# Loading the rows of decay sums into tiles of their own, one group ahead

## The chip, the cores and the metric

The kernel runs on one core of a Trainium2 chip. The metric is the device time of one execution in microseconds (us). Three executions of the kernel before took 1480.74, 1482.68 and 2030.02 us; their median is 1482.68 us. The profiled execution took 1480.76 us.

## The reference

Two layers, each a SwiGLU feed-forward at half step, a mixing block, and a second feed-forward. The sequence has 256 positions, the model 1024 channels, all in float32. The mixing block runs an SSD branch (32 heads of 64 channels, 4 groups that share B and C) and a latent attention branch (8 heads) on the same input. What the change touches is the decay of the SSD branch:

```python
acum = jnp.cumsum(dtc * a_g, axis=1)
seg = acum[:, :, None] - acum[:, None, :]
decay = jnp.exp(jnp.where(causal, seg, -jnp.inf))
cb = jnp.einsum('btgn,bsgn->btsg', cc, bc)
xdt = xc * dtc[..., None]
y_diag = jnp.einsum('btsg,btsgh,bsghp->btghp', cb, decay, xdt)
```

The kernel treats the 256 positions as two blocks of 128 without a carried state: the matrix of decays between position s (on the partitions) and position t (along the free axis) has a 128x256 part for s in the first block and a 128x128 part for s in the second, 384 columns together.

## The kernel before, in words

Weights stream from HBM in blocks of up to 128x1024 (`ahead`, L144 to L155): SyncE loads a block into `st`, ScalarE rounds it to a high part `wh` (L152), VectorE forms the rest `wl` (L153), and TensorE multiplies with both. Four blocks are kept ahead. ScalarE therefore stands in the way of every weight block, beside all activations; it takes its instructions strictly in order, and so do the other engines. A wait at the head of ScalarE's queue holds back the roundings of later blocks, the activations of the convolutions and the softmax of attention.

The order of instructions on each engine is set when the program is built: `schedule_with_timeline_sim=True` (L904) lets a planner go through the program with costs of its own and place each instruction where its model says that it can start. A changed wait moves instructions on all engines in the mixing stage.

The mixing stage (`mix`, L418) computes the running sums `acum` (L529), turns them so that each head is a row, copies the 32 rows into `aT` (L535, L536: the 256 sums, and the last 128 once more), writes them to a DRAM tensor `rows` (L538) from GpSimd's queue, and goes through `loop_order` (L130): eight rounds j = 0 to 7, each with a pair of xs convolutions, `ssd(j)`, one attention head `head(j)`, and at every second round B and C of a group (`bc`), `query` and `keyval`.

`spread(j)` (L618) loads the rows of the four heads of round j, two heads at a time, spread over all partitions, into tiles `dec` of 128x2x384, of which there are two. Both loads stand on GpSimd's queue, which has nothing else to do in this stage. `ssd(j)` (L627) then works in place: ScalarE takes Relu of (own sum minus row) (L647, four instructions to a tile), then Exp (L648), VectorE multiplies with the masked C·B product `cbm` (L649), and TensorE multiplies with `xdt` (L655, 16 matmuls in a round). Only then are the tiles free, and `spread(j + 1)` follows at L657. A load of the next round thus waits for L655 of this round, and the Relus of the next round wait for the load.

Around it: `t` (L598) is the tanh of a convolution, `BC` (L599) its result for B and C, L606 the C·B product on TensorE, `cbm` (L609) its masked form. `peT` (L770) and `qkT` (L761, L762) are the operands of attention's scores, `pp` (L791) its probabilities, L802 the product with v. `tm` (L465) holds decay inputs and rotary keys after their transposition.

Of the kernel before, what the change touches and what calls it, by code (L numbers as in the profile page):

```python
# [11 lines left out]
F32 = mybir.dt.float32  # L12
# [3 lines left out]
AF = mybir.ActivationFunctionType  # L16
ALU = mybir.AluOpType

P = 128
L = 2  # L20
T = 256
# [5 lines left out]
NH = 32  # L27
# [33 lines left out]
class Build:  # L61
# [356 lines left out]
    def mix(self, l, X0, Xn, gain, gain_next):  # L418
        nc, v = self.nc, self.vec[l]
        tt, ts, stt = nc.vector.tensor_tensor, nc.vector.tensor_scalar, nc.vector.scalar_tensor_tensor  # L420
        act = nc.scalar.activation
# [40 lines left out]
        pt = self.sps()  # L462
        for c in range(2):
            nc.tensor.transpose(pt[:, c * P:(c + 1) * P], dk[:, c * P:(c + 1) * P], self.ident)
        tm = self.tmp("tm", [P, 2, P], bufs=1)  # L465
        for c in range(2):
            act(out=tm[:, c, :], in_=pt[:, c * P:(c + 1) * P], func=AF.Copy, scale=Rt[:, c:c + 1])
        latent(4)
# [42 lines left out]
        q = self.tmp("dtq", [P, 2, 32], bufs=1)  # L511
# [17 lines left out]
        acum = self.tmp("acum", [P, 2, 32], bufs=1)  # L529
        nc.vector.tensor_copy(acum, pa[:, :64].rearrange("p (c h) -> p c h", c=2))  # L530
        pT = self.sps()
        for c in range(2):
            nc.tensor.transpose(pT[:32, c * P:(c + 1) * P], acum[:, c, :], self.ident)
        aT = self.tmp("aT", [P, 3 * P], bufs=1)[:32]
        nc.scalar.copy(aT[:, :T], pT[:32, :T])  # L535
        nc.scalar.copy(aT[:, T:], pT[:32, P:T])  # L536
        rows = self.dram.tile([NH, 3 * P], F32, name=f"rows{l}")
        nc.gpsimd.dma_start(rows, aT)  # L538

        S = dict(l=l, X=X, A=A, acum=acum, rows=rows, dth=dth, Rf2=Rf2, ef=ef, Rfac=Rfac,  # L540
                 Rckv=Rc[:, 2:4], kpr=kpr, v=v)
# [75 lines left out]

    def spread(self, S, j):  # L618

        S["dec"] = []  # L620
        for q in range(2):
            h = 4 * j + 2 * q
            r = self.tmp("dec", [P, 2, 3 * P])
            self.nc.gpsimd.dma_start(r, S["rows"][h:h + 2, :].unsqueeze(0).to_broadcast([P, 2, 3 * P]))
            S["dec"].append(r)

    def ssd(self, S, j):  # L627
        nc = self.nc
        tt = nc.vector.tensor_tensor
        act = nc.scalar.activation  # L630
        xs, cbm = S["xs", j], S["bc", j // 2]
        h0 = 4 * j
        px = self.sps()
        for c in range(2):
            for i in range(2):
                nc.tensor.transpose(px[:, c * T + i * P:c * T + (i + 1) * P], xs[:, i, c * P:(c + 1) * P], self.ident)
        xdt = self.tmp("xdt", [P, 2, T], bufs=1)
        for c in range(2):
            tt(out=xdt[:, c, :].rearrange("p (h d) -> p h d", d=64),
               in0=px[:, c * T:(c + 1) * T].rearrange("p (h d) -> p h d", d=64),  # L640
               in1=S["dth"][:, c, h0:h0 + 4].unsqueeze(2).to_broadcast([P, 4, 64]), op=ALU.mult)
        dec = S["dec"]
        for q, r in enumerate(dec):
            for i in range(2):
                h = h0 + 2 * q + i
                for c, o, n in ((0, 0, T), (1, T, P)):
                    act(out=r[:, i, o:o + n], in_=r[:, i, o:o + n], func=AF.Relu, scale=-1.0, bias=S["acum"][:, c, h:h + 1])  # L647
            act(out=r, in_=r, func=AF.Exp, scale=-1.0)  # L648
            tt(out=r, in0=r, in1=cbm.unsqueeze(1).to_broadcast([P, 2, 3 * P]), op=ALU.mult)  # L649
        py = self.sps()  # L650
        for q, r in enumerate(dec):
            for c, o, n in ((0, 0, T), (1, T, P)):
                for i in range(2):
                    f = (2 * q + i) * 64
                    nc.tensor.matmul(py[64 * i:64 * i + 64, q * T + c * P:(q + 1) * T], lhsT=xdt[:, c, f:f + 64],  # L655
                                     rhs=r[:, i, o:o + n], start=q == 0 and c == 0, stop=q == 1 and c == 1)
        if j < 7:  # L657
            self.spread(S, j + 1)
        yv = self.tmp("yv", [P, 2, T], bufs=1)
        for i in range(2):  # L660
            nc.vector.scalar_tensor_tensor(out=yv[:, i, :], in0=xs[:, i, :], scalar=self.Dh[:, 2 * j + i:2 * j + i + 1],
                                           in1=py[:, i * T:(i + 1) * T], op0=ALU.mult, op1=ALU.add)
        S["yv", j] = yv
# [245 lines left out]
```

## Time and profile before

| | |
|---|---|
| profiled execution | 1480.76 us |
| its span | 1479.0 us |
| TensorE busy | 1452.7 us (98%) |
| VectorE busy | 1115.0 us (75%) |
| ScalarE busy | 912.0 us (62%) |
| GpSimd busy | 18.6 us (1%) |
| mixing stage of the first layer | about 220 to 475 us |
| mixing stage of the second layer | about 940 to 1210 us |

TensorE works through nearly the whole span. Its idle time and its clock are what a change can win back or lose, so the waits of TensorE and the granted clock (PEclk) are read first, and from each gap one goes back to what was late.

### The profile page before, as it was taken

What the parts mean: (1) busy time and instruction counts of PE and PEld (TensorE: products, weight loads), DVE (VectorE), ACT (ScalarE), POOL (GpSimd) and SP (SyncE); (2) the same over time, 40 slices, a digit from 0 to 9 for tenths busy, and PEclk for the clock granted to TensorE, in tenths of its full rate; (3) what the DMA queues carried; (4) which work ended last, traced back from release to release, by engine and by line L of the source; (5) the groups of instructions that cost most, each with busy time, mean ns of one, the idle gap of its engine ahead of it and who ended that gap; (6) DMA issues with size and microseconds to landing.
All of it is one profiled execution on the core that took longest, in us unless ns stands there. A gap on an engine that the chain in (4) does not pass through costs nothing.

```text
span 1479.0 us, 24986 instructions
## 1 busy us (share of the span) xinstructions
PE 1452.7 (98%) x9418; PEld 1305.6 (88%) x9418; DVE 1115.0 (75%) x2080; ACT 912.0 (62%) x1740; POOL 18.6 (1%) x38
## 2 busy tenths in 40 slices
PE   7999999999999999999999999999899999999999
PEld 6888899888888998888888888998798899988888
DVE  7887678977867677777677776889786776787764
ACT  6655566987875456555455554779777654555542
POOL 0000000000000000000000000000000000000000
PEclk9999999999999999999999999999999999999999
DMA  7555655544544655556655566556444555555563
GB/s 261 188 192 168 206 178 189 179 157 132 185 154 157 200 179 186 190 188 184 194 189 189 192 180 195 175 184 192 139 160 138 164 178 186 185 184 190 192 193 111
DMA packets 75977, 265.65 MB, mean 180 GB/s; under 512 B 8880, under 2 KB 11184, under 8 KB 75856
## 3 DMA queue, kind: packets, MB, share of 16 engines
q1 hardware_dynamic: 73232, 251.37, 52.6%
q0 software_dynamic: 2624, 12.68, 2.7%
q8 instruction: 74, 1.21, 0.3%
q14 instruction: 47, 0.39, 0.1%
HBM read 262.87 MB, written 1.15 MB: 179 GB/s over the span
## 4 chain that ended last, share of the span: by engine, by line
PE 87%; DVE 4%; issue 4%; DMA 3%; ACT 2%; POOL 0%; SPq 0%; POOLq 0%; ACTq 0%; DVEq 0%
PE g L178 40%; PE g L179 20%; PE g L169 7%; PE g L170 7%; PE g L171 7%; DMA dec<-rows 2%; DVE wl L153 1%; PE g L694 1%; PE s L655 1%; PE h L779 1%; PE g L718 1%; DVE cy L595 1%; PE h L778 1%; ACT dec L647 1%; ACT wh L152 1%
## 5 line engine op out<-in xcount | busy, mean ns | idle before, releaser
L152 ACT CAST wh<-st 128x1024 fp32r<-128x1024 f32 (+2 forms) x488 | 500.7, 1027 | 475.4 <-PE g L178 309.9
L153 DVE TENSOR_TENSOR wl<-st,wh 128x1024 fp32r<-128x1024 f32 (+2 forms) x488 | 581.3, 1192 | 261.6 <-ACT wh L152 257.9
L178 PE MATMUL g<-X,wh 128*128 128x512 f32 x928 | 326.5, 395 | 7.8 <-DVE X L205 7.4
L178 PE MATMUL g<-A,wh 128*128 128x512 f32 x938 | 327.6, 395 | 0.0
L179 PE MATMUL g<-X,wl 128*128 128x256 f32 x928 | 261.4, 282 | 0.5 <-DVE wl L153 0.5
L179 PE MATMUL g<-A,wl 128*128 128x256 f32 x938 | 260.5, 278 | 0.0
L178 PE MATMUL g<-oT,wh 128*128 128x512 f32 x704 | 244.5, 392 | 0.0
L169 PE MATMUL g<-X,wh 128*128 128x256 f32 x768 | 221.8, 290 | 3.4 <-DVE cy L595 2.9
L170 PE MATMUL g<-X,wh 128*128 128x256 f32 x768 | 220.9, 288 | 0.0
L171 PE MATMUL g<-X,wl 128*128 128x256 f32 x768 | 220.1, 287 | 0.0
L178 PEld LDWEIGHTS g<-X,wh 128*128 128x128 f32 x928 | 174.3, 188 | 47.2 <-DVE X L205 8.1
L178 PEld LDWEIGHTS g<-A,wh 128*128 128x128 f32 x938 | 175.7, 188 | 40.1
L179 PE MATMUL g<-oT,wl 128*128 128x256 f32 x704 | 196.9, 280 | 0.0
L179 PEld LDWEIGHTS g<-X,wl 128*128 128x128 f32 x928 | 175.9, 190 | 1.6 <-DVE wl L153 0.8
L179 PEld LDWEIGHTS g<-A,wl 128*128 128x128 f32 x938 | 176.6, 188 | 0.4
L178 PEld LDWEIGHTS g<-oT,wh 128*128 128x128 f32 x704 | 131.6, 187 | 28.6
L169 PEld LDWEIGHTS g<-X,wh 128*128 128x128 f32 x768 | 148.6, 194 | 6.2 <-DVE cy L595 4.1
L170 PEld LDWEIGHTS g<-X,wh 128*128 128x128 f32 x768 | 149.0, 194 | 0.6 <-issue 0.5
L171 PEld LDWEIGHTS g<-X,wl 128*128 128x128 f32 x768 | 148.8, 194 | 0.5 <-issue 0.5
L179 PEld LDWEIGHTS g<-oT,wl 128*128 128x128 f32 x704 | 133.0, 189 | 0.2
L171 PE MATMUL g<-oT,wl 128*128 128x256 f32 x272 | 76.8, 285 | 0.0
L170 PE MATMUL g<-oT,wh 128*128 128x256 f32 x272 | 76.7, 283 | 0.0
(287 smaller groups left out, 1831.2 us busy)
## 6 DMA issues: line engine op xcount, KB each, us to landing
st<-in_w_dram SPq DMA_DIRECT2D x238, 512.0 KB, 4.4
st<-in_win_dram SPq DMA_DIRECT2D x124, 512.0 KB, 4.1
st<-in_wso_dram SPq DMA_DIRECT2D x32, 512.0 KB, 3.7
st<-in_w_dram SPq DMA_DIRECT2D x32, 384.0 KB, 3.2
dec<-rows POOLq DMA_DIRECT2D x32, 384.0 KB, 5.4
st<-in_wmo_dram SPq DMA_DIRECT2D x16, 512.0 KB, 3.5
st<-in_wo_dram SPq DMA_DIRECT2D x16, 512.0 KB, 3.4
st<-in_wuq_dram SPq DMA_DIRECT2D x16, 384.0 KB, 3.2
```

Of the source, the lines that this page charges most:

```text
L152: self.nc.scalar.copy(wh, st)
L153: self.nc.vector.tensor_tensor(out=wl, in0=st, in1=wh.bitcast(F32), op=ALU.subtract)
L169: mm(out, lhsT=wh[:, k, :], rhs=xh, start=start and k == 0, stop=False)
L170: mm(out, lhsT=wh[:, k, :], rhs=xl, start=False, stop=False)
L171: mm(out, lhsT=wl[:, k, :], rhs=xh, start=False, stop=stop and k == nk - 1)
L178: mm(out, lhsT=wh[:, k, :], rhs=X[:, x0 + k, :], start=start and k == 0, stop=False)
L179: mm(out[:, :T], lhsT=wl[:, k, :], rhs=X[:, x0 + k, :T], start=False, stop=stop and k == nk - 1)
L595: nc.vector.scalar_tensor_tensor(out=y[:, i, k:], in0=ps[:, :T - k], scalar=v[:, w0 + 3 - k:w0 + 4 - k], in1=y[:, i, k:], op0=ALU.mult, op ...
L647: act(out=r[:, i, o:o + n], in_=r[:, i, o:o + n], func=AF.Relu, scale=-1.0, bias=S["acum"][:, c, h:h + 1])
L655: nc.tensor.matmul(py[64 * i:64 * i + 64, q * T + c * P:(q + 1) * T], lhsT=xdt[:, c, f:f + 64], rhs=r[:, i, o:o + n], start=q == 0 and c = ...
L694: nc.tensor.matmul(pc[c], lhsT=aa, rhs=ww, start=k == 0 and i == 0, stop=k == 3 and i == 2)
L718: nc.tensor.matmul(pc[c], lhsT=aa, rhs=ww[:, k, :], start=k == 0 and i == 0, stop=k == 1 and i == 2)
```

## The change

The rows of round j + 1 no longer land in the tiles in which round j still computes. They land in two tiles `row` of 128x2x256. ScalarE's Relus read `row` and write `dec`, and `spread(j + 1)` stands right behind the activations and multiplications of round j, ahead of its matmuls. A load now waits only for the Relus that read its tile. The Relus themselves, which write `dec`, now wait for the matmuls of the round before, where the load did so earlier. The rows are 256 long in place of 384; the Relu of the second part reads columns 128 to 255 of the same row. Two scratch tiles are dropped: `tm` uses the buffer of `qkT`, `aT` that of `pp`.

```diff
-        tm = self.tmp("tm", [P, 2, P], bufs=1)
+        tm = self.tmp("qkT", [P, 2, T], bufs=1)[:, :, :P]
...
-        aT = self.tmp("aT", [P, 3 * P], bufs=1)[:32]
-        nc.scalar.copy(aT[:, :T], pT[:32, :T])
-        nc.scalar.copy(aT[:, T:], pT[:32, P:T])
-        rows = self.dram.tile([NH, 3 * P], F32, name=f"rows{l}")
+        aT = self.tmp("pp", [P, 3 * P], bufs=1)[:NH, :T]
+        nc.scalar.copy(aT, pT[:NH, :T])
+        rows = self.dram.tile([NH, T], F32, name=f"rows{l}")
...
-        S["dec"] = []
+        S["row"] = []
         for q in range(2):
             h = 4 * j + 2 * q
-            r = self.tmp("dec", [P, 2, 3 * P])
-            self.nc.gpsimd.dma_start(r, S["rows"][h:h + 2, :].unsqueeze(0).to_broadcast([P, 2, 3 * P]))
-            S["dec"].append(r)
+            r = self.tmp("row", [P, 2, T])
+            self.nc.gpsimd.dma_start(r, S["rows"][h:h + 2, :].unsqueeze(0).to_broadcast([P, 2, T]))
+            S["row"].append(r)
...
-        dec = S["dec"]
-        for q, r in enumerate(dec):
+        dec = []
+        for q, row in enumerate(S["row"]):
+            r = self.tmp("dec", [P, 2, 3 * P])
+            dec.append(r)
             for i in range(2):
                 h = h0 + 2 * q + i
                 for c, o, n in ((0, 0, T), (1, T, P)):
-                    act(out=r[:, i, o:o + n], in_=r[:, i, o:o + n], func=AF.Relu, scale=-1.0, bias=S["acum"][:, c, h:h + 1])
+                    act(out=r[:, i, o:o + n], in_=row[:, i, c * P:], func=AF.Relu, scale=-1.0, bias=S["acum"][:, c, h:h + 1])
             act(out=r, in_=r, func=AF.Exp, scale=-1.0)
             tt(out=r, in0=r, in1=cbm.unsqueeze(1).to_broadcast([P, 2, 3 * P]), op=ALU.mult)
+        if j < 7:
+            self.spread(S, j + 1)
...
-        if j < 7:
-            self.spread(S, j + 1)
```

The planner then moves instructions in the mixing stages. Three places matter below. In the changed kernel the lines from L536 on stand one to three numbers off: the Relu is L648, Exp L649, the matmuls of `ssd` L658, tanh L597, `peT` L771, attention's scores L779 to L781.

First place: ScalarE's order around the Relus of round 4 in the first layer, with what each instruction waits for (PE, DVE, Activation: an engine; DMASW: a load from GpSimd's queue; DMAHW: one from SyncE's). Before:

```order
L703 COPY qn<-g 128x256
L770 COPY peT<-h 128x512 [waits PE_49]
L647 ACTIVATE dec<-dec,acum 128x256 [waits DMASW1_49]
...
L647 ACTIVATE dec<-dec,acum 128x256 [waits DMASW2_49]
...
L648 ACTIVATE dec<-dec 128x768 [waits Activation_49]
L598 ACTIVATE t_3770<-cy 128x512 [waits DVE_49]
L648 ACTIVATE dec<-dec 128x768 [waits Activation_49]
```

And in the changed kernel:

```order
L771 COPY peT<-h 128x512 [waits PE_49]
L682 ACTIVATE zz<-zz 128x512 [waits DVE_49]
L703 ACTIVATE ta,ss<-g 128x192 [waits Activation_49] x2
L704 COPY qn<-g 128x256
L152 CAST wh<-st 128x1024 [waits DMAHW0_49,PE_49]
L591 ACTIVATE cy<-g,vec_87 128x256 [waits PE_49]
L597 ACTIVATE t_3777<-cy 128x512 [waits DVE_49]
L648 ACTIVATE dec<-row,acum 128x256 [waits DMASW1_49,PE_49]
...
L648 ACTIVATE dec<-row,acum 128x256 [waits DMASW2_49,PE_49]
...
L649 ACTIVATE dec<-dec 128x768 [waits Activation_49] x2
```

The tanh `t` of B and C and one rounding `wh`, which stood behind the Relus, now stand ahead of them; the Relus wait for TensorE too.

Second place: TensorE's order at the attention head of round 3 in the first layer, around the matmuls of `ssd(3)`. Before:

```order
L655 MATMUL s<-dec,xdt 64x256 x2
L655 MATMUL s<-dec,xdt 64x128 x2
L769 MATMUL h<-cb,qp 128x128 x2
L769 MATMUL h<-cb,kp 128x128 x2
L778 MATMUL h<-qkT 128x128
L779 MATMUL h<-peT 128x128
L778 MATMUL h<-qkT 128x256
```

And in the changed kernel (24 matmuls of one weight block stand where the dots are):

```order
L770 MATMUL h<-cb,qp 128x128 x2
L770 MATMUL h<-cb,kp 128x128 x2
L779 MATMUL h<-qkT 128x128
L169 MATMUL g<-X,wh 128x256
...
L171 MATMUL g<-X,wl 128x256
L780 MATMUL h<-peT 128x128
L779 MATMUL h<-qkT 128x256
L780 MATMUL h<-peT 128x256
L781 LDWEIGHTS identb
L781 MATMUL h<-negb,identb 128x2x128
L658 MATMUL s<-dec,xdt 64x256 x2
```

The matmuls of `ssd(3)` moved from ahead of the attention scores to behind them, and a weight block's matmuls came in ahead of the first one that needs `peT`.

Third place: ScalarE's order at the first Relus of the first layer. Before:

```order
L152 CAST wh<-st 128x1024 [waits DMAHW4_49,PE_49]
L592 ACTIVATE cy<-g,vec_87 128x256 [waits PE_49]
L152 CAST wh<-st 128x768 [waits DMAHW5_49,PE_49]
L647 ACTIVATE dec<-dec,acum 128x256 [waits DMASW1_49]
L647 ACTIVATE dec<-dec,acum 128x128
```

And in the changed kernel:

```order
L152 CAST wh<-st 128x1024 [waits DMAHW4_49,PE_49]
L591 ACTIVATE cy<-g,vec_87 128x256 [waits PE_49]
L648 ACTIVATE dec<-row,acum 128x256 [waits DMASW1_49]
L648 ACTIVATE dec<-row,acum 128x128
L648 ACTIVATE dec<-row,acum 128x256
L648 ACTIVATE dec<-row,acum 128x128
L152 CAST wh<-st 128x768 [waits DMAHW5_49,PE_49]
```

One rounding of a weight block for `query` fell behind the first four Relus.

## Rows read from the trace of the kernel before

**Rows 1.** The page: busy time of the engines, share of the span, instructions.

```profile
PE 1452.7 (98%) x9418; PEld 1305.6 (88%) x9418; DVE 1115.0 (75%) x2080; ACT 912.0 (62%) x1740; POOL 18.6 (1%) x38
```

**Rows 2.** Waits of TensorE: releaser, us in total, times, longest us.

```profile
PE s L606 <- DVE BC L599: 4.4, 2, 3.5
PE h L802 <- ACT pT L800: 3.3, 1, 3.3
PE g L169 <- DVE cy L595: 2.9, 2, 2.4
```

**Rows 3.** Timeline of TensorE: start, us, operation [idle before it <- releaser].

```profile
320.69 0.49 PE L778 MATMUL h<-qkT 128*128 128x128 f32 x2 [1.22 <-ACT peT L770]
330.02 0.70 PE L606 MATMUL s<-BC 128*128 128x256 f32 x2 [0.98 <-DVE BC L599]
337.13 0.70 PE L802 MATMUL h<-pT,vv 128*128 128x256 f32 x2 [3.33 <-ACT pT L800]
1060.80 0.70 PE L606 MATMUL s<-BC 128*128 128x256 f32 x2 [3.46 <-DVE BC L599]
1120.05 0.58 PE L169 MATMUL g<-X,wh 128*128 128x256 f32 x1 [2.37 <-DVE cy L595]
```

**Rows 4.** Busy time by stretch, granted clock (PEclk); the last stretch for comparison.

```profile
338.10:341.50 3.40, 3.40 (x18) 3.40 (x17) 3.28 (x11) 1.83 (x4) 0.00 (x0) 0.50 0.45 148
1061.80:1065.20 3.40, 3.40 (x16) 3.15 (x15) 2.63 (x5) 2.81 (x5) 0.00 (x0) 0.51 0.05 14
1119.80:1123.20 3.40, 3.15 (x15) 3.15 (x15) 3.40 (x8) 1.81 (x9) 0.00 (x0) 0.50 0.49 169
300.00:303.40 3.40, 3.40 (x31) 3.40 (x30) 3.22 (x7) 2.06 (x6) 0.00 (x0) 1.00 0.63 221
```

**Rows 5.** Timeline of ScalarE, Relus of round 4, first layer.

```profile
320.01 0.63 ACT L770 COPY peT<-h 128x512 f32<-128x512 f32 x1
324.72 1.49 ACT L647 ACTIVATE dec<-dec,acum 128x256 f32<-128x256 f32 x4 [4.08 <-DMA dec<-rows]
326.49 1.50 ACT L647 ACTIVATE dec<-dec,acum 128x256 f32<-128x256 f32 x4 [0.27 <-DMA dec<-rows]
328.63 0.61 ACT L598 ACTIVATE t<-cy 128x512 f32<-128x512 f32 x1
```

**Rows 6.** Timeline of VectorE behind it.

```profile
329.27 0.69 DVE L599 SCALAR_TENSOR_TENSOR BC<-t,cy 128x512 f32<-128x512 f32 x1 [4.45 <-ACT t L598]
```

**Rows 7.** Timeline of GpSimd's queue: the loads of round 4, first layer.

```profile
318.21 1.19 POOL L624 DMA_DIRECT2D dec<-rows  x2 [18.86 <-PE s L655]
```

**Rows 8.** Tile dec: time from issue to landing of its 32 loads.

```profile
DMA to landing us min/median/max: 3.6/5.4/8.0
```

**Rows 9.** Waits of ScalarE for these loads, both layers.

```profile
ACT dec L647 <- DMA dec<-rows: 22.1, 14, 4.3
```

**Rows 10.** Timeline of ScalarE, other Relus, rounds 0 and 1, then second layer.

```profile
255.49 3.11 ACT L647 ACTIVATE dec<-dec,acum 128x256 f32<-128x256 f32 x8 [2.91 <-DMA dec<-rows]
266.88 1.50 ACT L647 ACTIVATE dec<-dec,acum 128x256 f32<-128x256 f32 x4
1055.14 1.49 ACT L647 ACTIVATE dec<-dec,acum 128x256 f32<-128x256 f32 x4 [4.30 <-DMA dec<-rows]
1109.80 0.80 ACT L647 ACTIVATE dec<-dec,acum 128x256 f32<-128x256 f32 x2 [0.31 <-DMA dec<-rows]
```

**Rows 11.** Busy time by stretch around the first loads of the first layer.

```profile
240.00:260.00 20.00, 20.00 (x168) 19.78 (x166) 15.56 (x45) 12.30 (x26) 1.72 (x3) 1.00 0.56 173
```

**Rows 12.** Timeline of TensorE: a round's L655, and attention's scores from first to last.

```profile
317.03 1.52 PE L655 MATMUL s<-dec,xdt 128*64 128x256 f32 x16
321.11 0.48 PE L779 MATMUL h<-peT 64*128 64x128 f32 x2
322.78 0.28 PE L780 MATMUL h<-negb,identb 128*128 128x256 bf16 x1
```

**Rows 13.** The page's groups: the roundings of weights, busy us, mean ns | idle before.

```profile
L152 ACT CAST wh<-st 128x1024 fp32r<-128x1024 f32 (+2 forms) x488 | 500.7, 1027 | 475.4 <-PE g L178 309.9
```

## The prediction

> **What bounds the kernel now.** The page comes first: TensorE is busy for 1452.7 us of the span of 1479.0 [rows 1], GpSimd's 18.6 us are only the issuing of loads, and ScalarE and VectorE, at 62% and 75%, have room on average. So little more than 26 us of TensorE's time is idle, and no change off TensorE can win much more than that and what the clock takes after a gap.
>
> The second view is the waits of TensorE [rows 2], the third its timeline, to see where they lie [rows 3]. The five largest gaps of the two mixing stages are 1.22, 0.98, 3.33, 3.46 and 2.37 us, together 11.4. Behind three of the places the granted clock is 0.50 for about 3.4 us, the lower of the two levels (1.2 in place of 2.4 GHz): TensorE had sat idle just before, and in such a stretch it ran 18, 16 and 15 matmuls where a stretch of the same length at full clock holds 31 [rows 4]. At half clock 3.4 us do the work of 1.7, so each place cost another 1.7 us. The granted clock is read off; the 1.7 is worked out from it.
>
> Then one goes back from a gap to what was late. In the first layer ScalarE finishes `peT` at about 320.6 and stands still for 4.08 us, until the load for the Relus of round 4 has landed [rows 5]. That load was issued at 318.21, and what released it were the matmuls L655 of the round before [rows 7]. Behind the waiting Relu on the same queue stand Exp, the tanh `t` of B and C, the softmax and the roundings of weights. `t` runs at 328.63; VectorE, which waits 4.45 us for it, can finish `BC` only at 329.27 and on [rows 6]; TensorE's L606 waits for that, and later L802 for attention's `pT`. In the second layer the same round does the same: ScalarE waits 4.30 us [rows 10], L606 3.46 us [rows 3]. Over both layers ScalarE waits 22.1 us in 14 pieces for these loads [rows 9], but most pieces cost nothing: around the 2.91 us at 255 [rows 10] TensorE was busy for 20.00 of 20 us [rows 11]. The four roundings ahead cover a wait of that size, not one of 4.1. The border lies between.
>
> **The change, part by part.**
>
> Earlier loads. A load now waits for the Relus of its own round, not for the matmuls behind them. Landing takes 3.6 to 8.0 us [rows 8], and from the first round's Relus to the second's, which are the closest, there are 11.4 (255.49 to 266.88 [rows 10]). So from round 1 on the rows lie ready, and the wait for the load goes. What ScalarE waits for next is the matmuls of the round before, which must have read `dec`. The Relu can start the moment these end, 5 us earlier than before at the median.
>
> The price, gap by gap:
> - First layer, round 4: 0.98 + 3.33 = 4.31 us, and 1.7 of clock: 6.0.
> - Second layer, round 4: 3.46 + 1.7 = 5.2. In the changed order `t` stands ahead of the Relus at both places, so `BC` no longer waits for them at all.
> - Second layer, the gap at 1120: 2.37 + 1.7 = 4.1. Here ScalarE waited only 0.31 us for the load [rows 10]; the rest was a dense sequence of Relus, softmax and roundings. I count half: 2.0. Its ends are 0 and 4.1.
> - First layer, `peT`: the wait of 1.22 us [rows 3] goes, because a weight block's 24 matmuls now stand ahead of the first use of `peT`. At 31 in 3.4 us [rows 4], 24 take 2.6 us, more than the wait: 1.2.
>
> Together 14.4 us.
>
> The Trainium skill (DMA: Bandwidth & Descriptors, section on the anatomy of a DMA on the gpsimd path) gives a fixed part of about 2.0 us and 436 KB per us after that. An estimate from that page makes 2.9 us for a load of 384 KB, so that the load issued at 318.21 would be there at about 321.1; ScalarE would have waited half a microsecond, no gap of round 4 would be this load's doing, and the sum would be near 3 us. No load of this kernel was that quick: 3.6 us at the least, 5.4 at the median [rows 8], and the sum above goes by them.
>
> The Relus' new wait. It now stands on ScalarE's queue, where it holds back everything, and not on GpSimd's, where nothing was behind it. Its cost isn't in the trace, so I bound it. Below: 0, if the matmuls are always done. Above: the wait of 4.3 us that a load caused [rows 10]. At round 4 of the first layer the order gives a middle: from the start of `peT` TensorE has 24 matmuls (2.6 us), the scores from L779 on (321.11 to 322.78, 1.7 us) and L658 (1.5 us) [rows 12], 5.8 together. ScalarE has `peT` and `t` (0.6 each [rows 5]), a rounding (1.0 [rows 13]) and five activations and copies, which I put at 0.37 each, a Relu's share of four in 1.49 [rows 5]: 4.1. The difference is about 1.7 us, nearer to the 2.91 that cost nothing than to the 4.08 that cost a gap. I take no gap here.
>
> New order. The planner moved instructions on three engines, and its model had let the old gaps happen too. For stalls that I can't name I take one gap like that at 1120 with its clock, 2.37 + 1.7 = 4.1 us; the ends are none and three.
>
> First loads. Nothing can be prefetched for round 0; the load is a third smaller. One rounding now stands behind the first four Relus, so it waits for the load too, some 4 us later than before. What covers it: its block is for `query`, whose matmuls come after the first L655, and TensorE was busy throughout [rows 11]. Cost nothing; if the cover were gone, up to 2.91 us.
>
> At nothing, too: the two short copies of 128 columns that fall away lie on ScalarE beside TensorE's work. The sharing of buffers adds waits for things long done: attention's first `qkT` and `pp` stand on ScalarE's queue behind the Relus of round 0, which need `tm` read and `rows` written. A Relu keeps its shape and its time. The traffic of these loads falls by a third, of an amount that GpSimd issued in 18.6 us.
>
> Sum: 14.4 - 4.1 = 10.3 us. From the profiled execution of 1480.76 us that gives 1470.5. The median of the runs shown, 1482.68, lies 1.9 us above that execution, so I round up to **1471 us**.
>
> **The rivals.**
>
> Nothing is left over (chance 0.20): the planner's new order opens gaps as large as those it closes. For it: the old gaps arose in an order that the same planner thought dense. Against: the long wait that set them off is gone from the queue. With three gaps of 4.1 us in place of one the gain is 14.4 - 12.3 = 2; time 1476 to 1484.
>
> Slower (0.13): ScalarE waits for L658 in place of the load. Place: the Relus of round 3 onward, whose predecessors now end behind attention's scores on TensorE (second place in the order). It decides from about 3 us on, between 2.91 and 4.08. Two such stalls in each layer, each costing 3.4 us of gap and 1.7 of clock, are 20.4 us; less the 14.4 gained, and with the 4.1 of the new order, +10: 1491, and up to 1500 with a third. My 1.7 us at round 4 speaks against it, but not from far off.
>
> The change doesn't take effect (0.02): the loads would still be issued late. GpSimd's order in the changed kernel shows loads that wait for ScalarE and for loads, and no longer for TensorE or VectorE; so I give this little. Time 1479 to 1483.
>
> My forecast has 0.65: one to four of the gaps gone, 1463 to 1476. Its low end takes all of rows 3 and three times 1.7, 11.4 + 5.1 = 16.5, which gives 1464.3, and one microsecond for waits too short to be seen in a view of idle time.
>
> **Range and chances.** 1463 to 1485 takes in the forecast, the case without gain and the third case, 0.87, less what each loses beyond its ends; about 8 in 10. Two per cent, about what a measurement of this kernel can tell from no change, are 30 us. To be faster by that, more than all idle time of TensorE would have to go: 0.01. To be slower by that, the third rival would have to come three times as strong: 0.03. Within 2%: 0.96.
>
> **What would show it.** In the changed profile: the wait of ScalarE's Relus for loads falls from 22.1 us to the first round of each layer, 4 to 6 us in all; the loads' releaser is ScalarE; `BC` no longer waits over 4 us for `t`; L606 has no gap above 1 us in round 4 of either layer; the stretches at half clock fall from three to one or none. It is wrong if ScalarE's Relus show waits for L658 above 3 us with TensorE idle behind them, or if gaps of 2 us and more turn up at other lines, most likely at scores, L803 or the convolutions' first matmuls.

## The result, and the profile after

The changed kernel takes 1467.62 us (median of four runs, 1466.14 to 1469.72), the kernel before 1482.68 us (median of its three undisturbed runs, 1480.74, 1482.68 and 1485.76; one of 2030.02 us is left out). The ratio is 0.9897, with a 95% interval of 0.9871 to 0.9923, so the change gains 15 us. The profiled execution of the changed kernel is the longest of its four, 1469.72 us, 11.0 us below that of the kernel before.

The page, busy time of the changed kernel by engine (the row that answers to [rows 1]):

```profile
PE 1451.8 (99%) x9418; PEld 1304.8 (89%) x9418; DVE 1114.6 (76%) x2080; ACT 911.8 (62%) x1738; POOL 18.5 (1%) x38
```

No engine does noticeably less. What changed is idle time. The table of stretches shows where; its columns are those of [rows 4], and the two rows are the mixing stages of the two layers. Before:

```profile
220.00:475.00 255.00, 247.86 (x1775) 224.40 (x1774) 201.79 (x442) 193.07 (x434) 9.24 (x17) 0.99 0.51 167
940.00:1210.00 270.00, 262.74 (x1880) 238.49 (x1880) 215.08 (x467) 203.76 (x450) 9.13 (x17) 0.99 0.51 168
```

After:

```profile
220.00:475.00 255.00, 252.81 (x1820) 229.88 (x1819) 208.47 (x458) 198.01 (x439) 9.22 (x17) 0.99 0.51 163
940.00:1210.00 270.00, 267.65 (x1933) 243.65 (x1932) 221.19 (x477) 206.40 (x452) 9.11 (x17) 1.00 0.51 164
```

In the same time TensorE did 45 and 53 matmuls more. Its idle time is the width of a stretch less the first busy column: 7.14 + 7.26 = 14.4 us before, 2.19 + 2.35 = 4.5 after, 9.9 us less.

TensorE's waits after (engine, line, what it waited for: us in total, times, longest), to be held against [rows 2]:

```profile
PE g L178 <- DVE X L205: 7.5, 2, 7.0
PE g L719 <- DVE sm L794: 2.2, 1, 2.2
PE g L169 <- DVE cy L594: 1.2, 2, 0.9
PE g L719 <- DVE cy L594: 1.1, 1, 1.1
```

The waits for `BC`, for `pT` and for `peT` are gone from the list. The first row lies outside the mixing stages and was there before. The other three are new, and the timeline shows where they lie (start and duration in us; in brackets the idle time ahead):

```profile
285.73 0.76 PE L719 MATMUL g<-wh,A 128*128 128x512 f32 x1 [2.19 <-DVE sm L794]
...
1010.01 0.47 PE L719 MATMUL g<-wh,A 128*128 128x512 f32 x1 [1.13 <-DVE cy L594]
...
1013.23 0.39 PE L169 MATMUL g<-X,wh 128*128 128x256 f32 x1 [0.94 <-DVE cy L594]
```

Round 4, where the chain of the prediction ran, has no gap in either layer, and none is left at 1120 but for 0.21 us.

ScalarE's waits at the Relus after:

```profile
ACT dec L648 <- DMA row<-rows: 4.5, 2, 3.6
ACT dec L648 <- PE s L658: 4.2, 4, 2.2
```

And GpSimd's, the releaser of the loads, with the time from issue to landing from the view of the tile `row`:

```profile
POOL row L623 <- ACT dec L648: 230.1, 28, 26.4
```

```profile
DMA to landing us min/median/max: 3.3/3.9/4.9
```

ScalarE stands still for loads for 4.5 us instead of 22.1 [rows 9], twice, once in the first round of each layer. GpSimd's 230 us are waits with nothing behind them. ScalarE's timeline at the first Relu, at round 3 and at round 4 of the first layer:

```profile
257.76 1.49 ACT L648 ACTIVATE dec<-row,acum 128x256 f32<-128x256 f32 x4 [3.58 <-DMA row<-rows]
...
301.43 2.88 ACT L648 ACTIVATE dec<-row,acum 128x256 f32<-128x256 f32 x8 [2.19 <-PE s L658]
...
328.31 0.62 ACT L597 ACTIVATE t<-cy 128x512 f32<-128x512 f32 x1
...
329.71 2.88 ACT L648 ACTIVATE dec<-row,acum 128x256 f32<-128x256 f32 x8 [0.78 <-PE s L658]
```

And VectorE's `BC`, which waited 4.45 us for `t` before [rows 6]:

```profile
330.24 0.68 DVE L598 SCALAR_TENSOR_TENSOR BC<-t,cy 128x512 f32<-128x512 f32 x1
```

`BC` waits for nothing. The Relus of both tiles now run as one group of eight.

The stretches around the one gap that took clock with it, and the stretch before it:

```profile
265.00:285.60 20.60, 18.53 (x129) 15.62 (x126) 20.22 (x41) 20.60 (x51) 1.61 (x3) 1.00 0.62 196
285.60:289.00 3.40, 3.27 (x9) 2.72 (x10) 3.21 (x9) 3.40 (x12) 0.54 (x1) 0.50 0.58 202
```

Behind the 2.19 us at 285.73 TensorE was granted 0.50, 1.2 GHz, for 3.4 us. It is the only such stretch in the mixing stages, at a place where there was none before; behind the three places of [rows 4] the clock no longer falls. In the 20.6 us ahead of it ScalarE was busy throughout and VectorE for 20.22 us; the matmul L719 starts when VectorE has worked off `sm`.

So the profiled execution gains 9.9 us of idle time and two stretches of half clock at 1.7 us, 13.3 together. Its difference is 11.0. The missing 2.3 us are of the size by which the matmuls of the feed-forward stages, which the change doesn't touch, differ between executions (the last section). More than that is lost ahead of the first mixing stage: the second product of the first feed-forward (L178 with `A`) starts at 137.4 us, where it started at 133.8 before, and at 135.9 in the repeated run of the change.

### The profile page after: what moved, and what is told of

Its sections match the earlier page's. It is cut to its first block, busy times and chain, and to the rows that moved or that the text cites. A ratio compares the mean times of both kernels' runs of the same rounds, so it can differ in the third digit from the quotient of the medians.

```text
span 1467.8 us, 25011 instructions
## 1 busy us (share of the span) xinstructions
PE 1451.8 (99%) x9418; PEld 1304.8 (89%) x9418; DVE 1114.6 (76%) x2080; ACT 911.8 (62%) x1738; POOL 18.5 (1%) x38
## 4 chain that ended last, share of the span: by engine, by line
PE 97%; DVE 1%; ACT 1%; issue 0%; DMA 0%; SPq 0%; DVEq 0%; ACTq 0%
PE g L178 40%; PE g L179 21%; PE g L169 9%; PE g L170 9%; PE g L171 9%; PE g L695 2%; PE s L658 2%; PE g L719 1%; PE h L780 1%; PE h L779 1%; PE h L761 0%; PE s L635 0%; PE h L803 0%; DVE wl L153 0%; DVE cy L594 0%; PE h L799 0%
## 5 line engine op out<-in xcount | busy, mean ns | idle before, releaser
L178 PE MATMUL g<-X,wh 128*128 128x512 f32 x928 | 330.8, 399 | 8.0 <-DVE X L205 7.5
L178 PE MATMUL g<-A,wh 128*128 128x512 f32 x938 | 327.6, 395 | 0.0
L178 PE MATMUL g<-oT,wh 128*128 128x512 f32 x704 | 244.5, 392 | 0.0
L169 PE MATMUL g<-X,wh 128*128 128x256 f32 x768 | 219.6, 287 | 1.2 <-DVE cy L594 1.2
L178 PEld LDWEIGHTS g<-X,wh 128*128 128x128 f32 x928 | 175.8, 189 | 49.3 <-DVE X L205 8.3
L170 PE MATMUL g<-X,wh 128*128 128x256 f32 x768 | 218.7, 285 | 0.0
L178 PEld LDWEIGHTS g<-A,wh 128*128 128x128 f32 x938 | 175.7, 188 | 40.1
L178 PEld LDWEIGHTS g<-oT,wh 128*128 128x128 f32 x704 | 131.6, 187 | 28.6
L169 PEld LDWEIGHTS g<-X,wh 128*128 128x128 f32 x768 | 146.7, 191 | 3.2 <-issue 1.6
```

The costliest lines, as they stand in the source:

```text
L169: mm(out, lhsT=wh[:, k, :], rhs=xh, start=start and k == 0, stop=False)
L170: mm(out, lhsT=wh[:, k, :], rhs=xl, start=False, stop=False)
L178: mm(out, lhsT=wh[:, k, :], rhs=X[:, x0 + k, :], start=start and k == 0, stop=False)
```

## The experiments

Each is compared with the kernel before on the same chip. "Gain" is one minus the ratio, times 1482.68 us.

**Does the sharing of buffers, or the place in the program, count?** First the sharing alone, on the kernel before.

```diff
-        tm = self.tmp("tm", [P, 2, P], bufs=1)
+        tm = self.tmp("qkT", [P, 2, T], bufs=1)[:, :, :P]
...
-        aT = self.tmp("aT", [P, 3 * P], bufs=1)[:32]
+        aT = self.tmp("pp", [P, 3 * P], bufs=1)[:32]
```

> The kernel before with only the two scratch tiles put into the buffers of qkT and pp. All expect no difference: within 2 us of before, the same gaps at the same places.

Ratio 1.0004 (0.999 to 1.0019): no difference. Then the changed kernel with `spread(j + 1)` put back behind the matmuls, its tiles kept:

```diff
-        if j < 7:
-            self.spread(S, j + 1)
         py = self.sps()
...
+        if j < 7:
+            self.spread(S, j + 1)
```

> The changed kernel with the call of spread back behind the round's matmuls in the program; the load's semaphores still wait for the Relus alone. If the freed wait is what pays and not the place in the program: as the changed kernel, 13 to 17 us faster than before. If the place in the program matters: less than 10 us faster.

Ratio 0.9885 (0.9863 to 0.9908), 1467.32 us: the same as the change. What counts is the tile that a load writes into, not the line at which it is written down.

**The size alone.** The kernel before with rows of 256 (and one copy of 256 columns to write them), loaded in place; the second part's Relu runs first, and the loads still wait for the matmuls.

```diff
...
-            self.nc.gpsimd.dma_start(r, S["rows"][h:h + 2, :].unsqueeze(0).to_broadcast([P, 2, 3 * P]))
+            self.nc.gpsimd.dma_start(r[:, :, :T], S["rows"][h:h + 2, :].unsqueeze(0).to_broadcast([P, 2, T]))
...
-                for c, o, n in ((0, 0, T), (1, T, P)):
-                    act(out=r[:, i, o:o + n], in_=r[:, i, o:o + n], func=AF.Relu, scale=-1.0, bias=S["acum"][:, c, h:h + 1])
+                for c, o, n in ((1, T, P), (0, 0, T)):
+                    act(out=r[:, i, o:o + n], in_=r[:, i, c * P:T], func=AF.Relu, scale=-1.0, bias=S["acum"][:, c, h:h + 1])
```

> The kernel before with rows of 256 in place of 384, loaded into the first 256 columns of dec, the second part's Relus first; the load still waits for the matmuls of the round before. If the early issue is what pays: the load lands about 1.5 us sooner (3.9 us in the changed kernel against 5.4), ScalarE's waits for loads fall from 22 to 10 to 14 us, the 4.1 us waits to about 2.7, and a part of the gaps goes: 3 to 8 us faster than before. If the smaller load is the whole gain: 13 to 16 us faster, like the changed kernel. If the size is of no account: within 2 us of before.

Ratio 0.9954 (0.994 to 0.9968): a gain of 6.8 us. ScalarE waits for loads even longer than before, 25.0 us in 17 pieces, where 10 to 14 were expected; the gain came anyway. At round 4 of the first layer its timeline reads:

```profile
322.30 0.60 ACT L769 COPY peT<-h 128x512 f32<-128x512 f32 x1
...
326.60 0.40 ACT L646 ACTIVATE dec<-dec,acum 128x128 f32<-128x128 f32 x1 [3.12 <-DMA dec<-rows]
326.91 0.61 ACT L597 ACTIVATE t<-cy 128x512 f32<-128x512 f32 x1
```

The wait is still 3.12 us, but `t` stands behind one short Relu instead of all of them, and starts 4.6 us after `peT` where it was 8.6 [rows 5]. TensorE has no gap here. So this edit changes an order, too, and the size of the loads isn't separated from it. TensorE's longest gap is elsewhere, in attention:

```profile
1062.93 0.70 PE L801 MATMUL h<-pT,vv 128*128 128x256 f32 x2 [2.21 <-ACT pT L799]
```

**The order alone.** The kernel before, its Relus held on ScalarE's queue behind the tanh of B and C; loads as before.

```diff
-        nc.scalar.activation(out=th, in_=y, func=AF.Tanh, scale=0.5)
+        t = nc.scalar.activation(out=th, in_=y, func=AF.Tanh, scale=0.5).ins
+        if key == "bc":
+            self.tanh = t
...
+                  with self.tc.issue_after(self.tanh):
                     act(out=r[:, i, o:o + n], in_=r[:, i, o:o + n], func=AF.Relu, scale=-1.0, bias=S["acum"][:, c, h:h + 1])
```

> The kernel before, loads and tiles unchanged, but the Relus are queued on ScalarE behind the tanh of the latest B and C. If the order alone made the gain: the waits for loads stay near 22 us and the time is 10 to 16 us below before. If the waiting of ScalarE is the cause: VectorE and the matmuls L606 no longer wait for B and C (0.98 and 3.46 us and some of the clock), but attention's gap of 3.3 us stays: 3 to 8 us faster than before.

Ratio 0.9934 (0.991 to 0.9958): a gain of 9.8 us, between the two expectations. ScalarE's waits for loads are 18.7 us in 15 pieces, the longest 2.6. At round 4 of the first layer `t` now fills a part of what was waiting before:

```profile
322.63 0.63 ACT L598 ACTIVATE t<-cy 128x512 f32<-128x512 f32 x1 [1.92 <-DVE cy L595]
...
325.00 1.49 ACT L650 ACTIVATE dec<-dec,acum 128x256 f32<-128x256 f32 x4 [1.74 <-DMA dec<-rows]
```

TensorE's waits:

```profile
PE h L781 <- ACT peT L773: 2.5, 2, 1.2
PE h L805 <- ACT pT L803: 1.8, 1, 1.8
```

The two gaps at `BC` are gone; both waits for `peT` stay, and one gap at `pT`. So some two thirds of the gain can be had without an earlier load, by what stands ahead of the waiting Relu.

**Both, still in place.** The last two edits together.

> In place, late loads, but rows of 256 and the Relus queued behind the tanh of B and C: both cheaper remedies together, each of which alone gave a part (about 7 and 10 us). If what counts is only that ScalarE's waits stay under the three or so us that the roundings cover: nearly the whole gain without an early load, 11 to 16 us faster than before. If the early load gives something of its own: 7 to 11 us faster, and 5 us or more behind the changed kernel.

Ratio 0.9919 (0.9895 to 0.9943): a gain of 12.0 us. ScalarE still waits 20.8 us for loads. The changed kernel once more, on the same chip:

> The changed kernel itself, beside the other on the same chip: 14 to 17 us faster than before.

Ratio 0.9899 (0.988 to 0.9917); the medians are 1470.94 and 1467.24 us. The two intervals overlap, but by these medians the change is worth 3.7 us beyond size and order. The traces put them into the clock and not into idle time: TensorE is idle for 4.8 us in the mixing stages in place and for 4.6 with the change, but in place two stretches run at half clock, at 1.7 us each, and with the change none:

```profile
372.50:376.50 4.00, 4.00 (x16) 2.85 (x16) 3.78 (x15) 1.48 (x4) 0.00 (x0) 0.57 0.77 251
1028.40:1031.80 3.40, 3.37 (x16) 3.40 (x17) 2.41 (x5) 2.87 (x10) 0.00 (x0) 0.53 0.53 159
```

The mean granted clock says the same of all four executions: 0.997 or 0.998 in place, 0.999 or 1.000 with the change. The gaps ahead of the two stretches, 1.24 us at `peT` and 1.87 us at L169, are not shown to come from a load: in the 15 us ahead of each ScalarE waits for none. So the 3.7 us can't be put down to the earlier loads. The parts don't add up: 6.8 and 9.8 make 12.0, since both edits clear the same gaps, those at `BC`, the one at 337.13 and the one at 1120.05 [rows 3].

**Own tiles, loads late.** The changed kernel, its loads held until VectorE has read the result of the round's matmuls.

```diff
-        if j < 7:
-            self.spread(S, j + 1)
         py = self.sps()
...
+        late = self.tmp("krs", [P, 2], bufs=1)[:, :1]
+        for row in S["row"]:
+            tt(out=late, in0=py[:, 2 * T - 1:2 * T], in1=row[:, 0, :1], op=ALU.add)
+        if j < 7:
+            self.spread(S, j + 1)
```

> The changed kernel with its own row tiles and rows of 256, but each load is held until the round's matmuls are done, by a one-column addition on VectorE that reads the result of the matmuls and the row tile (32 small instructions more). If the early issue is what pays: ScalarE waits for the loads again, 10 to 25 us in all, and 6 to 15 us of the gain of 15 are lost: 0 to 9 us faster than before. If separate tiles, the smaller load or the new order are what pays: 13 to 16 us faster still.

Ratio 0.9966 (0.995 to 0.9982): a gain of 5.0 us, 10 less than the change. ScalarE's and TensorE's waits:

```profile
ACT dec L648 <- DMA row<-rows: 23.0, 15, 4.0
```

```profile
PE g L169 <- DVE rqt L223: 4.4, 2, 2.2
PE s L635 <- DVE xs L598: 2.7, 2, 1.4
PE s L656 <- DVE dec L650: 2.4, 2, 1.3
```

Tiles of their own and smaller rows with the loads late bring no more than smaller rows alone; the waits of before are back, with gaps at other lines. The chain of the kernel before shows again, two rounds earlier: a Relu waits for its load, `t` stands behind it (at 294.32), VectorE waits for `t`, and TensorE's L635 for `xs`, at 295.71 after 1.41 us idle:

```profile
292.92 1.49 ACT L648 ACTIVATE dec<-row,acum 128x256 f32<-128x256 f32 x4 [3.96 <-DMA row<-rows]
```

```profile
294.96 0.69 DVE L598 SCALAR_TENSOR_TENSOR xs<-t,cy 128x512 f32<-128x512 f32 x1 [4.46 <-ACT t L597]
```

So late loads do cost TensorE time. How much of the 15 us is theirs isn't separated: this edit adds two short VectorE instructions to a round and ties the loads to VectorE's reading of the result, which the kernel before did not, so the 10 us may be more than the loads' earliness alone.

**One row tile instead of two.** The changed kernel with `bufs=1`: the second load of a round can't be prefetched.

```diff
-            r = self.tmp("row", [P, 2, T])
+            r = self.tmp("row", [P, 2, T], bufs=1)
```

> The changed kernel with one row tile in place of two: the second load of a round waits for the first tile's Relus, so about 3 us of waiting stand between the two tiles' Relus of a round. If waits of ScalarE up to about 3 us are covered by the four roundings ahead: ScalarE's waits for loads rise to 20 to 45 us, but TensorE's idle time rises by less than 5 us: 8 to 15 us faster than before. If every wait of ScalarE for a load costs TensorE: no faster than before, 0 to 20 us slower.

Ratio 0.9947 (0.9926 to 0.9968): a gain of 7.9 us, half of the change's and just under the 8 to 15 of the first expectation. ScalarE waits only 10.9 us for loads in 10 pieces (20 to 45 were expected), none over 2.8 us. Yet gaps open. In round 1 ScalarE waits first, then TensorE; TensorE's second row is a later gap, which isn't traced back:

```profile
268.12 0.51 ACT L648 ACTIVATE dec<-row,acum 128x256 f32<-128x256 f32 x1 [1.94 <-DMA row<-rows]
```

```profile
275.43 0.49 PE L779 MATMUL h<-qkT 128*128 128x128 f32 x2 [1.92 <-ACT qkT L763]
...
343.54 0.49 PE L779 MATMUL h<-qkT 128*128 128x128 f32 x2 [1.64 <-ACT qkT L763]
```

```profile
276.20:283.00 6.80, 6.80 (x29) 4.82 (x28) 4.57 (x13) 6.39 (x18) 0.54 (x1) 0.55 0.38 131
```

The chain of waits runs from the load to the Relu, on to `qkT` behind it, to L779. ScalarE has no idle time between the Relu and `qkT`, so its wait of 1.94 us reaches TensorE, which loses 1.92 us; the stretch behind was granted 0.55.

**Three tiles in place.** The kernel before with a third `dec` tile, so that one load of each round can start a round early, the other not; the sharing of buffers and the place of `spread` are those of the change.

```diff
...
-            r = self.tmp("dec", [P, 2, 3 * P])
+            r = self.tmp("dec", [P, 2, 3 * P], bufs=3)
...
```

> The kernel before, in place with rows of 384, but with three dec tiles and spread ahead of the matmuls: the first load of the next round goes out early, the second when the first tile's matmuls are done. If the early issue is what pays, whatever the tiles: ScalarE's waits fall to a half or less and the time is 5 to 14 us below before. If the separate tiles or the smaller load are needed: within 3 us of before.

Ratio 1.0098 (1.007 to 1.0126): 14.5 us slower, and no expectation held. ScalarE's waits at the Relus, and its timeline at round 4 of the first layer:

```profile
ACT dec L647 <- DMA dec<-rows: 29.8, 14, 7.2
```

```profile
329.61 1.49 ACT L647 ACTIVATE dec<-dec,acum 128x256 f32<-128x256 f32 x4 [4.86 <-DMA dec<-rows]
...
331.63 0.47 ACT L762 ACTIVATE qkT<-h,vec 128x256 f32<-128x256 f32 x1
```

TensorE there and after:

```profile
332.14 0.64 PE L769 MATMUL h<-cb,qp 128*128 128x128 f32 x2 [2.34 <-ACT qkT L762]
...
343.49 0.77 PE L718 MATMUL g<-wh,A 128*128 128x512 f32 x1 [2.67 <-DVE rob L356]
...
348.62 0.48 PE L798 MATMUL h<-cb,pp 128*128 128x128 f32 x1 [2.24 <-ACT pp L795]
```

The late load of a round now makes ScalarE wait for up to 7.2 us, and `qkT` right behind the Relus is late for TensorE. That the planner put Relus further ahead, since it thought the loads early, is my reading of the order; no run separates it.

**The gap that is left.** The changed kernel, with the additions of squares moved from VectorE to GpSimd, since VectorE was full ahead of the gap at 285.73.

```diff
-            nc.vector.tensor_tensor(out=self.accs, in0=self.accs, in1=z, op=ALU.add)
+            nc.gpsimd.tensor_tensor(out=self.accs, in0=self.accs, in1=z, op=ALU.add)
```

> The changed kernel with the 14 additions of squares (128x512, about 0.68 us each on VectorE) on GpSimd. If what is left of TensorE's gaps in the mixing stages comes from a full VectorE: 1 to 4 us faster than the changed kernel. If GpSimd's slower work or a load behind it on its queue costs more: the same or up to 10 us slower than the changed kernel.

Ratio 0.9888 (0.9862 to 0.9913): the same as the change, and the gap stays, at 2.5 us. None of those additions lies ahead of it in this layer, so the run doesn't test the reason. That VectorE and ScalarE are full there is seen, that this is the cause is not shown.

Not tried: rows of 384 in tiles of their own, and the change without shared scratch.

**All runs together.** The first column of numbers is TensorE's idle time in the two mixing stages (220 to 475 and 940 to 1210 us) of the profiled execution, the second the stretches at half clock in them. "Worked out" is the idle time and 1.7 us for each stretch, taken from the 19.5 us that the kernel before loses so.

| run | idle, us | half clock | gain worked out, us | gain measured, us |
|---|---|---|---|---|
| before | 14.4 | 3 | | |
| the change | 4.5 | 1 | 13.3 | 15 |
| the change once more | 4.6 | 0 | 14.9 | 15.0 |
| `spread` behind the matmuls | 4.3 | 0 | 15.2 | 17.1 |
| sums on GpSimd | 5.6 | 0 | 13.9 | 16.6 |
| both, in place | 4.8 | 2 | 11.3 | 12.0 |
| order alone | 5.8 | 1 | 12.0 | 9.8 |
| one row tile | 7.2 | 3 | 7.2 | 7.9 |
| size alone | 7.1 | 3 | 7.3 | 6.8 |
| own tiles, loads late | 10.1 | 3 | 4.3 | 5.0 |
| sharing alone | 13.6 | 3 | 0.8 | -0.6 |
| three tiles in place | 23.0 | 7 | -15.4 | -14.5 |

Within 3 us, every gain and loss is idle time and clock of TensorE in the mixing stages. Each edit also makes the planner order the instructions anew, so no run changes one wait alone.

## Why the prediction was right, point by point

The forecast was 1471 us and its likeliest case, part of the gaps gone; the time is 1467.62 us, 3.4 below and inside the range. For the profiled execution the sum gave 1470.5, and it was 1469.72. That these two lie within 0.8 us is partly luck: the mixing stages gave 3.0 us more than the sum has, and 2.3 us were lost outside of them.

**What bounds.** Right. All that was won is idle time of TensorE and its clock. But the "five largest gaps" are not the five largest. The prediction overlooked the second wait for `peT`, in the second layer, which is longer than two of its five:

```profile
1050.89 0.49 PE L778 MATMUL h<-qkT 128*128 128x128 f32 x2 [1.24 <-ACT peT L770]
```

**Earlier loads.** Right in mechanism and size: waits of ScalarE for loads 4.5 us (4 to 6 said), only in round 0 of each layer, the loads released by ScalarE. The price behind it is more mixed than "the load was late". Three runs with 20 us and more of waiting for loads differ by 7 us in their time (gains of 5.0, 6.8 and 12.0 with 23.0, 25.0 and 20.8 us). In these three the longest wait after round 0 (4.0, 3.3 and 1.9 us) does go with the loss; that length alone doesn't decide either is shown under "The border".

**Round 4 in both layers, 6.0 + 5.2.** Right, with the step that the prediction named: `t` ahead of the Relus frees `BC`. Holding that order alone gained 9.8 us, without touching a load.

**The gap at 1120, counted half at 2.0.** Mis-sized: it went but for 0.21 us. A single loss of 2.37 us of gap, with 1.7 of clock, ended as a whole, so the half was the wrong value between right ends. It also went with the size alone and with the order alone, where the loads are late, so the earlier load isn't needed for it; what caused it is not shown.

**`peT`, 1.2.** Too small: both waits for it went, 1.22 and 1.24 us, where only the first layer's was counted. With the order alone both stay, which speaks for the weight block that the change puts ahead of them.

**The Relus' new wait.** Right, though the estimate was twice too long: 0.78 us at round 4 (1.7 estimated), 2.19 us at its longest, at round 3, and no gap of TensorE behind any. The rival that made the kernel slower through these waits falls.

**The border, "between 2.91 and 4.08".** Wrong as a rule. With one row tile, in round 1 and with ScalarE full behind it, 1.94 us cost a gap; with smaller rows in place, at round 4 with one short Relu in front of `t`, 3.12 us cost none. The kernel before has a wait of the same 1.94 us, with no gap of TensorE in the 30 us behind it:

```profile
1086.75 1.49 ACT L647 ACTIVATE dec<-dec,acum 128x256 f32<-128x256 f32 x4 [1.94 <-DMA dec<-rows]
```

There is no such number; there is only the slack at that place. In the changed kernel this didn't matter, since the waits came where there was slack.

**New order, one gap of 4.1.** Right in kind, half as large again in the profiled execution: 2.19 + 1.13 + 0.94 + 0.21 = 4.5 us and one half-clock stretch, 6.2; the repeated run has 4.6 us without the stretch. None of the three gaps is at a place that the prediction named as likely. Two are at L719, within the weight block of `keyval`, and one at L169, at a block of `z`; two of the three wait for `cy`, VectorE's part of a convolution.

**Its signs.** All the signs of being right came. So did one of the signs of being wrong, by its letter: a gap of 2 us or more at another line, the 2.19 at L719 (1.82 in the repeated run, 1.62 with `spread` behind the matmuls). The sign was drawn too tight, since the sum itself counts one new gap of 2.37 us. ScalarE's waits for L658 above 3 us did not come.

**First loads, the sharing, the shorter rows.** Nothing, nothing, and more than nothing. The 3.58 us at the first Relu cost no gap. The sharing is 1.0004. The rows' size was counted at nothing; in place, and with the new order of the Relus that came with it, it is worth 6.8 us. On top of the order alone it adds 2.2 us (12.0 less 9.8), not clear of noise, and no run shows what it adds on top of the earlier loads.

Together: the mixing stages had 14.4 us of idle time and 5.1 of lost clock, and have 4.5 and 1.7 in the profiled execution, 4.6 and nothing in the repeated one. That is 13.3 and 14.9 us won, where the sum had 10.3. Ahead of what the new order costs, 19.5 us were there to win and nearly all of them went, which the prediction kept for its low end; it counted 14.4. The other half of the gap at 1120 (2.1), the second wait for `peT` (1.2) and short waits (1.8) make the difference. What the new order costs was too small by 2.1 us in the profiled execution and by 0.5 in the repeated one.

An estimate worked out from the Trainium skill (DMA: Bandwidth & Descriptors, the anatomy of a DMA on the gpsimd path) is 2.6 us for a load of 256 KB. It was 3.3 us at the least and 3.9 at the median, as with the longer rows above the page's figure. The sum of near 3 us that the page led to did not come.

## What to carry to other kernels

A tile that a load fills and that is then computed in place ties the load to the last reader of the result; a landing tile of its own ties it to the first instruction alone, and the wait moves from the engine in front of the load to a queue with nothing behind it. Don't price a wait on an in-order queue by its length: look at the instructions behind it, and first ask whether the urgent one can stand ahead, which here brought two thirds of the gain without an earlier load. A third tile for loads and results in place, which lets only some of the loads start early, was the one edit here that made the kernel slower.

## What the runs showed of the hardware

A gap doesn't tell by its length whether the clock falls. Behind the 1.22 us at 320.69 in the kernel before the granted clock stayed at 1.00 for the next 3.4 us:

```profile
320.70:324.10 3.40, 3.40 (x20) 2.50 (x21) 3.40 (x12) 0.00 (x0) 0.00 (x0) 1.00 0.93 290
```

And behind the 3.33 us at 337.13 it fell to 0.50 [rows 4]. With the sharing of buffers alone, the same two gaps were followed by the opposite: the clock fell behind the short one and not behind the long one.

```profile
323.08 0.49 PE L778 MATMUL h<-qkT 128*128 128x128 f32 x2 [1.23 <-ACT peT L770]
...
339.96 0.70 PE L802 MATMUL h<-pT,vv 128*128 128x256 f32 x2 [3.30 <-ACT pT L800]
```

```profile
324.00:328.00 4.00, 4.00 (x16) 2.96 (x17) 2.93 (x13) 0.42 (x2) 0.00 (x0) 0.57 0.88 337
340.00:343.40 3.40, 3.40 (x27) 3.35 (x28) 3.37 (x10) 1.29 (x4) 0.00 (x0) 1.00 0.45 147
```

The changed kernel itself has the gap before L719 at half clock in one execution, and in the repeated one, where it is 1.82 us, at 1.00 (with the sums on GpSimd it is 2.51 us, and the clock doesn't fall there either):

```profile
283.80:287.20 3.40, 2.96 (x17) 2.42 (x18) 3.20 (x8) 3.40 (x12) 0.54 (x1) 1.00 0.67 206
```

The same 928 matmuls of the feed-forward stages vary too. Before, and after (the page's groups: busy us, mean ns of one, idle time ahead):

```profile
L178 PE MATMUL g<-X,wh 128*128 128x512 f32 x928 | 326.5, 395 | 7.8 <-DVE X L205 7.4
```

```profile
L178 PE MATMUL g<-X,wh 128*128 128x512 f32 x928 | 330.8, 399 | 8.0 <-DVE X L205 7.5
```

In the repetition of the change they took 328.7 us. That is 2 to 4 us between executions, with 2.1 of it between two of the same kernel, as much as the smaller terms of this sum.
